# Moving operand splits, a butterfly step and gate copies between engines, and re-ordering the Fourier and gate stages of a hybrid GLA + Fourier encoder layer

## The chip, the cores and the metric

The kernel runs on one core of a Trainium2 chip. The metric is the device time of one execution in microseconds, the median of several. Five engines work side by side, each through its own instruction queue in order: PE (TensorE, matrix products), DVE (VectorE), ACT (ScalarE), POOL (GpSimd) and SP (SyncE, which here only starts DMAs).

## The reference, cut to what matters

```
proj = x @ w_in                      # 2048 x 1024 by 1024 x 2592
q, k, v, gf, gb, z_gla, u, z_fnet = split(proj)
log_a(dir) = log_sigmoid(g(dir) @ w_up(dir) + b(dir)) / 16
o = GLA_chunked(q, k, v, log_a fwd) + flip(GLA_chunked(flipped, log_a bwd))   # 4 heads
y_gla = rmsnorm(o) * g * silu(z_gla)
uf = real(fft2(u over positions and 128 channels of each of 4 groups)) @ w_fnet[group]
y_fnet = uf * silu(z_fnet)
out = layernorm(2**0.25 * x + concat(y_gla, y_fnet) @ w_out)
```

All data are float32. To keep precision each operand of a large product is held as a high part `hi` (rounded to the matmul's format) and a low part `lo = x - hi`, and each product is three matmuls: hi*hi, hi*lo, lo*hi.

## The kernel before, in words

The positions are cut into 8 blocks of 256 (`BLK`), the model width into 8 pieces of 128. Four phases follow one another.

Phase 1 projects `z_gla`, `u` and `z_fnet` (the last two by Strassen-like products, `run` and `product`, in the order of `LAST` for the last quarter) and writes them to DRAM scratch (`u_d`, `zf_d`, `zg_d`).

Phase 2 runs two generators side by side. `qk_all` goes through the 8 blocks: `load_x` loads x in two halves and splits it (`split`, lines 56 and 59: `hi` on ACT, `lo` on the engine given, here GpSimd), and `qk_block` makes four pieces ("qk steps") of 24 matmuls each (line 87), 32 steps in all. `fnet_pe` does the Fourier part for 4 groups of channels: `fft(g)` loads a 16 x 128 tile from `u_d`, and does a 16-point butterfly in the free dimension, almost all of it on DVE (lines 456 to 510; the subtraction of line 457 on GpSimd), ending in four splits into `bhl`; `stage2` (line 563) multiplies by the twiddle-and-DFT table `et`, `mixdown` (lines 575 to 590) by the channel matrices, and `gate_f` (line 598, on GpSimd) multiplies by `zf` and stores to `mf_d`. The transform of group 0, three pieces of that of group 1 and the loading of the table `et` stand ahead of the loop; the loop then lets the Fourier generator begin after `WARM` = 6 qk steps, and advances it twice a step. From step 18 on `wvg_load` loads and splits the weights of v and of the gate into the space that the Fourier tiles leave (`wA`), one piece per step (`hi` on ACT, line 655, `lo` on GpSimd, line 656).

Phase 3 makes v, the decay gates and the chunked attention, block by block. `pw_part` and `pv_part` (line 94, 24 matmuls each) project one half block; `gate_evac` copies the low-rank gate columns out of PSUM (lines 700 to 702) into `rn`; `gates` transposes `rn` (line 725), multiplies by the up-projection (line 733), takes log-sigmoid (lines 735 to 739), scans (744, 746), subtracts the middle of the chunk (750), clips (751), keeps small columns in `cmid`, `cend`, `cst` (755 to 759) and takes two exponentials (761, 762). `scaled` (777) applies these to q and k. `gla_a` (785 to 794) makes scores and transposed keys, masks them on DVE (`at`, lines 791 and 792); `gla_b` (802 to 810) makes the state updates and the inner output. A block's `gla_a` and `gla_b` run in the next block's turn. `chain_f` does the state recurrence on GpSimd (984, 987).

Phase 4 normalises, gates, projects out (line 1008) and does the LayerNorm; the change doesn't touch it.

Instructions are written in program order and assigned to their engine by the code; a planner then fixes the order within each engine's queue ahead of the run, by a list schedule in which program order is the priority and an estimate of readiness decides. `issue_after(i)` pins instructions behind `i` in their queue. Tiles with one tag share `bufs` buffers, so a load waits until the last reader of the buffer's previous content is done: `xraw` has 2 buffers, `xhl` 4, `wraw` 4.

Of the kernel before, what the change touches and what calls it, by code (L numbers as in the profile page):

```python
# [31 lines left out]
MID = 63  # L32
WARM = 6
LIMIT = 28.0
NS = 6
PRE = 3
LAST = ((0, 1), (0, 2), (0, 6), (0, 5), (0, 3), (1, 1), (1, 6), (0, 7), (0, 4), (1, 7), (1, 4), (1, 5), (1, 3), (1, 2))
CAP = (LIMIT + 1.0) * TAU
# [6 lines left out]
class Kern:  # L45
# [37 lines left out]
    def proj_t(self, ps, xh, w, c0):  # L83
        for k in range(KB):
            x = xh[k // 4]
            for i, (s, m) in enumerate(((0, 0), (0, 1), (1, 0))):
                self.nc.tensor.matmul(ps, w[:, s, k, c0:c0 + P], x[:, m, k % 4, :],  # L87
                                      start=(k == 0 and i == 0), stop=(k == KB - 1 and i == 2))

# [49 lines left out]
    def phase1(self):  # L139
# [3 lines left out]
        with ExitStack() as ctx:  # L143
# [252 lines left out]
            for p in range(NP):  # L396
                for _ in nxt:
                    pass
                nxt = x_prep(p + 1, xs[p + 1]) if p + 1 < NP else iter(())
                seq = both(p, (1, 2) + ORDER)  # L400
                if p == NP - 1:
                    seq = [(u, c, p) for u, c in LAST]
                for n, (u, c, _) in enumerate(seq):
                    run(u, c, p, xs[p])
                    if len(seq) - n in (9, 5, 3, 1):
                        next(nxt, None)
                    if p == NP - 1 and (u, c) == (0, 5):
                        self.wqk = self.load_w("wC", a["w_qk"], KB, 512)
                if p == 1:
                    self.consts()  # L410

    def consts(self):
# [20 lines left out]
    def phase2(self):  # L433
        nc, a = self.nc, self.a
        with ExitStack() as ctx:
# [10 lines left out]
            fw = self.wpool.tile([P, 56, P], F32, name="fw", tag="wA")  # L446

            def fft(g, out):
                V = nc.vector
                u = fw[:, 16 * (g % 2):16 * (g % 2) + 16]  # L450
                n = 4 if g == 0 else NCH
                for b in range(0, NCH, n):
                    nc.sync.dma_start(out=u[:, b:b + n], in_=self.u_d[:, b:b + n, g * P:(g + 1) * P])
                eo = fw[:, 32:48]
                tm = fw[:, 48:56]
                V.tensor_tensor(out=eo[:, 0:8], in0=u[:, 0:8], in1=u[:, 8:16], op=ALU.add)
                nc.gpsimd.tensor_tensor(out=eo[:, 8:16], in0=u[:, 0:8], in1=u[:, 8:16], op=ALU.subtract)
                yield
# [63 lines left out]

            bt0 = []
            for _ in fft(0, bt0):
                pass
            nb1 = []
            nf1 = fft(1, nb1)
            for _ in range(PRE):
                next(nf1)
            et = self.wpool.tile([P, 2, 9, 384], F32R, name="et", tag="wB")  # L530
            for k in range(9):
                raw = self.xpool.tile([P, 384], F32, name="eraw", tag="wraw", bufs=4)
                nc.sync.dma_start(out=raw, in_=a["etab"][:, k])
                self.split(et[:, 0, k], et[:, 1, k], raw)

            def qk_block(b, xh):
                for c0, d in ((256, self.kr_d[b]), (0, self.qr_d[b])):
                    ps = self.mm([P, 2, BLK])
                    for i in range(2):
                        self.proj_t(ps[:, i], xh, self.wqk, c0 + i * P)  # L540
                        if i == 0:
# [51 lines left out]
            def gate_f(g, yf):  # L593
                for b in range(NBLK):
                    zf = fp.tile([P, BLK], F32, name="zfl", tag="zfl", bufs=3)
                    nc.sync.dma_start(out=zf, in_=self.zf_d[b][:, g, :])
                    yb = yf[:, b * BLK:(b + 1) * BLK]
                    nc.gpsimd.tensor_tensor(out=yb, in0=yb, in1=zf, op=ALU.mult)
                    if b % 2:
# [3 lines left out]
            def fnet_pe():  # L603
                bt = bt0
                for _ in range(WARM):
                    yield
                pend = None
                for g in range(4):
# [4 lines left out]
                    for ks in ((1, 2), (3, 4), (5, 6), (7,), (0, 8)):  # L613
                        yhl = stage2(g, bt, ks)
                        next(nf, None)
# [14 lines left out]
            def qk_all():  # L630
                xn = self.load_x(0, nc.gpsimd)
                for b in range(NBLK):
                    xh = xn
                    if b + 1 < NBLK:
                        xn = self.load_x(b + 1, nc.gpsimd)
                    yield from qk_block(b, xh)

            ga, gb = qk_all(), fnet_pe()
            def wvg_load():
                w = self.wvg = self.wpool.tile([P, 2, KB, 544], F32R, name="wA_w", tag="wA")  # L640
                raws = []
                for k in range(KB + 4):
# [29 lines left out]
    def phase3(self):  # L672
# [16 lines left out]
        with ExitStack() as ctx:  # L689
# [28 lines left out]

            def gates(b, blk):
                rn = blk["rn"]  # L720
                tp = self.pg([P, 2, P])
                R = gp.tile([98, BLK], F32R, name="R", tag="R", bufs=1)
# [3 lines left out]
                nc.scalar.copy(out=R[0:96], in_=tp[0:96].rearrange("p t j -> p (t j)"))  # L726
                g = gp.tile([P, 4, BLK], F32, name="g", tag="g", bufs=2)
                zs = []
                for i in range(2):
# [24 lines left out]
                cs_ = slice(2 * b, 2 * b + 2)  # L754
                V.tensor_copy(out=cmid[:, cs_], in_=cv[:, :, :, MID])  # L755
                V.tensor_copy(out=cend[0:64, cs_], in_=gv[0:64, :, :, P - 1])
                V.tensor_copy(out=cend[64:128, cs_], in_=gv[64:128, :, :, 0])
                V.tensor_copy(out=cst[0:64, cs_], in_=gv[0:64, :, :, 0])
                V.tensor_copy(out=cst[64:128, cs_], in_=gv[64:128, :, :, P - 1])
                eq = c  # L760
# [62 lines left out]

            prev, xn = None, self.load_x(0, nc.gpsimd)
            for b in range(NBLK):
# [3 lines left out]
                pw_part(xh, 1, blk)  # L829
                gates(b, blk)  # L830
                qk_load(b, blk)
                if b + 1 < NBLK:
                    xn = self.load_x(b + 1, nc.gpsimd)
                if b < 2:
                    pv_part(xh, 0, blk)
                if b == 0:
                    pv_part(xh, 1, blk)
                if prev:
                    gla_a(b - 1, 0, prev)
                    if b > 1:  # L840
                        pv_part(xh, 0, blk)
                    gla_b(b - 1, 0, prev)
                scaled(blk)
# [324 lines left out]
```

## Time and profile before

| | |
|---|---|
| median of 3 runs | 863.68 us (863.08 to 865.26) |
| the profiled execution | 860.85 us, span of its instructions 859.1 us |
| PE busy | 788.5 us, 92% |
| DVE busy | 561.5 us, 65% |
| ACT busy | 381.7 us, 44% |
| POOL busy | 309.1 us, 36% |

Busy time is the time in which an engine executes; PE is counted busy at either level of its clock, which the profile gives as a granted share of full speed (1.00 is 2.4 GHz, 0.50 is 1.2 GHz, a value between is a mix in time). Times in the rows are microseconds from the span's start, mean durations are nanoseconds. "idle before <- X" names what ended an engine's idle time.

### The profile page before, as it was taken

To read this page: it belongs to the slowest core of one execution; us is meant where nothing else is said; L and a number is where in the kernel's file an instruction comes from. 1 tells how busy PE (TensorE), PEld (TensorE's weight loads), DVE (VectorE), ACT (ScalarE), POOL (GpSimd) and SP (SyncE) were. 2 spreads that over 40 slices of the span, in tenths; PEclk is the share of its full clock that TensorE was granted. 3 is DMA by queue.
4 is the path that set the end of the run, shared out by engine and by line. 5 is a ranking of instruction groups with operands and counts; after the bars stand their busy time and mean duration, and the time that the engine had idled before them with its cause. 6 is when DMAs were issued, how large, how long until landed. Compare 5 with 4: busy or idle time off the path is not lost. (4 is left out here: it accounts for less than half of the span.)

```text
span 859.1 us, 14088 instructions
## 1 busy us (share of the span) xinstructions
PE 788.5 (92%) x5542; PEld 737.1 (86%) x5542; DVE 561.5 (65%) x782; ACT 381.7 (44%) x668; POOL 309.1 (36%) x193
## 2 busy tenths in 40 slices
PE   7999999999999779799967979888988999999995
PEld 7999999999998769799966879887966788888885
DVE  5772377555458997642046788887796877677764
ACT  5864452332134234344244546545665444433441
POOL 0000003111123646357642464354344554455421
PEclk9999999999999789999978999898989999999998
DMA  8864345141338635366842543343448434554232
GB/s 246 276 221 129 110 151 175 64 143 62 118 123 257 203 126 169 121 192 198 235 148 74 147 130 114 91 141 117 123 133 284 167 134 150 186 196 147 89 109 78
DMA packets 75233, 130.51 MB, mean 152 GB/s; under 512 B 7219, under 2 KB 46643, under 8 KB 75158
## 3 DMA queue, kind: packets, MB, share of 16 engines
q1 hardware_dynamic: 72854, 125.34, 46.0%
q10 hardware_dynamic: 2304, 4.20, 1.4%
q8 instruction: 45, 0.74, 0.4%
q14 instruction: 30, 0.25, 0.1%
HBM read 92.81 MB, written 36.70 MB: 151 GB/s over the span
## 5 line engine op out<-in xcount | busy, mean ns | idle before, releaser
L94 PE MATMUL mm<-wA_w,xhl 128*128 128x272 f32 x768 | 111.6, 306 | 1.2 <-POOL xhl L59 1.2
L59 POOL TENSOR_TENSOR xhl<-xraw,xhl 128x1024 fp32r<-128x1024 f32 x32 | 83.9, 2626 | 73.1 <-ACT xhl L56 53.5
L94 PEld LDWEIGHTS mm<-wA_w,xhl 128*128 128x128 f32 x768 | 107.1, 205 | 1.7 <-POOL xhl L59 1.4
L87 PE MATMUL mm<-xhl,wC_w 128*128 128x256 f32 x768 | 101.5, 292 | 6.1 <-POOL xhl L59 6.1
L87 PEld LDWEIGHTS mm<-xhl,wC_w 128*128 128x128 f32 x768 | 98.7, 201 | 7.2 <-POOL xhl L59 6.6
L1008 PE MATMUL mm<-wB_w,mix 128*128 128x512 f32 (+1 forms) x396 | 94.6, 388 | 3.6 <-ACT mix L56 2.4
L1008 PE MATMUL mm<-wA_w,mix 128*128 128x512 f32 (+1 forms) x396 | 94.4, 391 | 2.1 <-ACT wA_w L56 2.1
L1008 PEld LDWEIGHTS mm<-wB_w,mix 128*128 128x128 f32 x396 | 73.1, 190 | 19.9 <-ACT mix L56 3.0
L984 POOL TENSOR_TENSOR S<-S 64x512 f32<-64x512 f32 x30 | 50.0, 1668 | 100.6 <-ACT S L804 94.8
L1008 PEld LDWEIGHTS mm<-wA_w,mix 128*128 128x128 f32 x396 | 72.3, 190 | 15.9 <-ACT wA_w L56 2.3
L87 PE MATMUL mm<-xhl,wA_w 128*128 128x256 f32 x672 | 81.3, 283 | 0.5 <-ACT zs L235 0.5
L87 PEld LDWEIGHTS mm<-xhl,wA_w 128*128 128x128 f32 x672 | 80.8, 192 | 1.1 <-ACT zs L235 0.7
L382 POOL TENSOR_TENSOR t<-t,t 128x512 f32<-128x512 f32 x7 | 11.0, 1576 | 191.8 <-ACT t L381 191.8
L56 ACT CAST xhl<-xraw 128x1024 fp32r<-128x1024 f32 (+1 forms) x54 | 51.4, 951 | 50.0 <-DMA xraw<-in_xt_dram 34.1
L1096 POOL TENSOR_TENSOR r<-r,lnb 128x1024 f32<-128x1024 f32 x15 | 35.8, 2387 | 78.2 <-issue 51.2
L59 DVE TENSOR_TENSOR x<-xraw,x 128x1024 fp32r<-128x1024 f32 x28 | 37.5, 1349 | 29.6 <-ACT x L56 29.6
L56 ACT CAST x<-xraw 128x1024 fp32r<-128x1024 f32 x28 | 29.0, 1047 | 44.2 <-PE mm L320 37.5
L320 PE MATMUL mm<-wC_s,x 128*128 128x256 f32 x384 | 48.2, 283 | 0.0
L320 PEld LDWEIGHTS mm<-wC_s,x 128*128 128x128 f32 x384 | 47.0, 192 | 0.0
L987 POOL TENSOR_TENSOR S<-S,alpha 64x512 f32<-64x512 f32 x30 | 44.5, 1483 | 2.3
L59 DVE TENSOR_TENSOR xhl<-xraw,xhl 128x1024 fp32r<-128x1024 f32 (+1 forms) x22 | 20.4, 932 | 28.6 <-ACT xhl L56 28.6
L320 PE MATMUL mm<-x,wB_s 128*128 128x256 f32 x288 | 36.5, 283 | 0.0
(183 smaller groups left out, 1520.5 us busy)
## 6 DMA issues: line engine op xcount, KB each, us to landing
xraw<-in_xt_dram SPq DMA_DIRECT2D x62, 512.0 KB, 4.6
xr<-in_x_dram SPq DMA_DIRECT2D x16, 512.0 KB, 3.7
out_dram<-r SPq DMA_DIRECT2D x15, 512.0 KB, 2.8
zg_d<-zs SPq DMA_DIRECT2D x32, 128.0 KB, 3.6
u_d<-t SPq DMA_DIRECT2D x16, 256.0 KB, 2.7
zf_d<-t SPq DMA_DIRECT2D x16, 256.0 KB, 2.1
zfl<-zf_d SPq DMA_DIRECT2D x32, 128.0 KB, 3.1
mf_d<-yf SPq DMA_DIRECT2D x16, 256.0 KB, 2.8
```

Source lines behind the costliest of these rows:

```text
L56: nc.scalar.copy(out=hi, in_=src)
L59: (lo_eng or nc.vector).tensor_tensor(out=lo, in0=src, in1=f32(hi), op=ALU.subtract)
L87: self.nc.tensor.matmul(ps, w[:, s, k, c0:c0 + P], x[:, m, k % 4, :], start=(k == 0 and i == 0), stop=(k == KB - 1 and i == 2))
L94: self.nc.tensor.matmul(ps, x[:, s, k % 4, t * P:(t + 1) * P], w[:, m, k, c0:c0 + cols], start=(k == 0 and i == 0), stop=(k == KB - 1 and ...
L320: nc.tensor.matmul(ps[:, i], s_[s][:, k, i * P:(i + 1) * P], m_[m][:, k], start=(k == 0 and j == 0), stop=(k == 3 and j == 2))
L382: G.tensor_tensor(out=T(3), in0=T(2), in1=T(0), op=ADD)
L984: E.tensor_tensor(out=S[ds, dst], in0=S[ds, dst], in1=S[ds, src], op=ALU.add)
L987: E.tensor_tensor(out=d3, in0=d3, in1=al, op=ALU.mult)
L1008: nc.tensor.matmul(y, c["mix"][:, s, eb], w[:, v, eb % 4, lo:lo + m], start=(eb == 4 and i == 0), stop=(eb == 3 and i == 2))
L1096: nc.gpsimd.tensor_tensor(out=r, in0=r, in1=lnb, op=ALU.add)
```

## The change

Five things change. (1) The `lo` halves of the splits of x in phases 2 and 3, the `lo` halves of the v and gate weights, the butterfly's subtraction and the gating of the last Fourier group go from GpSimd to VectorE. (2) Seven small copies per block of phase 3 go from VectorE to ScalarE. (3) The first transform and the loading of `et` are no longer ahead of the loop of phase 2: a generator `prelude` does them in pieces, two per step, beside `WARM` = 11 qk steps; their loads (`fft_load(0)`, `load_x(0)`) are issued in the last products of phase 1, two of which change places. (4) `stage2`'s matmuls are pinned behind the latest qk step's; the weights are loaded from step 24 on, two pieces a step, and the Fourier generator advances three times a step from step 27. (5) In phase 3 the transposes of `rn` become `gate_t`, and for blocks 2 to 7 the order is pw, pw, gla_a, gate_t, gla_b, gates, pv instead of pw, pw, transposes and gates, gla_a, pv, gla_b.

```diff
-WARM = 6
+WARM = 11
-PRE = 3
-LAST = (..., (1, 6), (0, 7), (0, 4), (1, 7), (1, 4), (1, 5), (1, 3), (1, 2))
+LAST = (..., (1, 6), (0, 7), (1, 7), (0, 4), (1, 4), (1, 5), (1, 3), (1, 2))
...
+                    if p == NP - 1 and (u, c) == (1, 4):
+                        self.fw = self.wpool.tile([P, 56, P], F32, name="fw", tag="wA")
+                        self.fft_load(0)
+                    if p == NP - 1 and (u, c) == (1, 3):
+                        self.x0 = self.load_x(0)
...
+    def fft_load(self, g):
+        u = self.fw[:, 16 * (g % 2):16 * (g % 2) + 16]
+        n = 4 if g == 0 else NCH
+        for b in range(0, NCH, n):
+            self.nc.sync.dma_start(out=u[:, b:b + n], in_=self.u_d[:, b:b + n, g * P:(g + 1) * P])
...
-                nc.gpsimd.tensor_tensor(out=eo[:, 8:16], in0=u[:, 0:8], in1=u[:, 8:16], op=ALU.subtract)
+                V.tensor_tensor(out=eo[:, 8:16], in0=u[:, 0:8], in1=u[:, 8:16], op=ALU.subtract)
...
-            for _ in fft(0, bt0):
-                pass
-            for _ in range(PRE):
-                next(nf1)
-            for k in range(9):
-                raw = self.xpool.tile([P, 384], F32, name="eraw", tag="wraw", bufs=4)
-                nc.sync.dma_start(out=raw, in_=a["etab"][:, k])
-                self.split(et[:, 0, k], et[:, 1, k], raw)
+            def et_load(ks):
+                for k in ks:
+                    raw = self.xpool.tile([P, 384], F32, name="eraw", tag="wraw", bufs=4)
+                    nc.sync.dma_start(out=raw, in_=a["etab"][:, k])
+                    self.split(et[:, 0, k], et[:, 1, k], raw)
+                    yield
+            def prelude():
+                yield from fft(0, bt0)
+                yield from et_load((1, 2, 3, 4, 5))
+                yield next(nf1)
+                yield from et_load((6, 7, 0, 8))
+                yield next(nf1)
+                yield next(nf1)
...
-                    nc.gpsimd.tensor_tensor(out=yb, in0=yb, in1=zf, op=ALU.mult)
+                    (nc.gpsimd if g < 3 else nc.vector).tensor_tensor(out=yb, in0=yb, in1=zf, op=ALU.mult)
...
+                pre = prelude()
                 for _ in range(WARM):
+                    next(pre, 0)
+                    next(pre, 0)
                     yield
+                for _ in pre:
+                    pass
...
-                        yhl = stage2(g, bt, ks)
+                        with self.tc.issue_after(self.qk_mm.ins):
+                            yhl = stage2(g, bt, ks)
...
-                xn = self.load_x(0, nc.gpsimd)
+                xn = self.x0
...
-                        xn = self.load_x(b + 1, nc.gpsimd)
+                        xn = self.load_x(b + 1)
...
-                        nc.gpsimd.tensor_tensor(out=lo, in0=raw, in1=f32(hi), op=ALU.subtract)
+                        nc.vector.tensor_tensor(out=lo, in0=raw, in1=f32(hi), op=ALU.subtract)
...
-                if step >= 18:
+                if step >= 24:
+                    next(gw, 0)
                     next(gw, 0)
...
-                for _ in range(2 if step > WARM else 1):
+                for _ in range(1 if step <= WARM else 2 if step < 27 else 3):
...
-                V.tensor_copy(out=rn[:, t, 64:96], in_=rn[:, t, 0:32])
+                nc.scalar.copy(out=rn[:, t, 64:96].bitcast(F32R), in_=sl)
...
-                V.tensor_copy(out=cmid[:, cs_], in_=cv[:, :, :, MID])
+                nc.scalar.copy(out=cmid[:, cs_], in_=cv[:, :, :, MID])
...
-            prev, xn = None, self.load_x(0, nc.gpsimd)
+            prev, xn = None, self.load_x(0)
...
-                gates(b, blk)
                 qk_load(b, blk)
                 if b + 1 < NBLK:
-                    xn = self.load_x(b + 1, nc.gpsimd)
-                if b < 2:
+                    xn = self.load_x(b + 1)
+                if b > 1:
+                    gla_a(b - 1, 0, prev)
+                    gate_t(blk)
+                    gla_b(b - 1, 0, prev)
+                    gates(b, blk)
                     pv_part(xh, 0, blk)
-                if b == 0:
-                    pv_part(xh, 1, blk)
-                if prev:
-                    gla_a(b - 1, 0, prev)
-                    if b > 1:
-                        pv_part(xh, 0, blk)
-                    gla_b(b - 1, 0, prev)
+                else:
+                    pv_part(xh, 0, blk)
+                    gate_t(blk)
+                    if b == 0:
+                        pv_part(xh, 1, blk)
+                    else:
+                        gla_a(b - 1, 0, prev)
+                        gla_b(b - 1, 0, prev)
+                    gates(b, blk)
                 scaled(blk)
```

(The copies to `cend` and `cst`, four a block, change engine like that to `cmid`. `gate_t` holds the transposes and the copy of `R` that stood at the head of `gates`.)

## Rows read from the trace of the kernel before

**Rows 1.** The page's first part: busy us, share of the span, instructions.

```profile
PE 788.5 (92%) x5542; PEld 737.1 (86%) x5542; DVE 561.5 (65%) x782; ACT 381.7 (44%) x668; POOL 309.1 (36%) x193
```

**Rows 2.** Busy time by stage: PE, PEld, DVE, ACT, POOL, then PEclk, DMA share, GB/s.

```profile
264.60:350.00 85.40, 68.71 (x499) 66.10 (x498) 79.67 (x156) 30.39 (x52) 45.03 (x21) 0.89 0.57 181
264.60:421.50 156.90, 140.15 (x1086) 137.40 (x1085) 103.50 (x204) 61.44 (x107) 86.70 (x58) 0.93 0.59 181
421.50:438.25 16.75, 7.55 (x52) 6.39 (x50) 1.27 (x6) 3.94 (x8) 12.51 (x14) 0.87 0.78 234
438.25:489.60 51.35, 44.32 (x288) 41.22 (x288) 36.66 (x44) 23.54 (x45) 18.24 (x8) 0.84 0.35 110
489.60:514.90 25.30, 20.93 (x176) 19.67 (x175) 21.28 (x24) 14.22 (x27) 13.08 (x6) 1.00 0.40 117
489.60:615.80 126.20, 113.26 (x871) 106.42 (x870) 103.57 (x122) 70.27 (x135) 57.54 (x28) 0.92 0.41 121
615.80:637.00 21.20, 16.99 (x135) 15.39 (x134) 19.05 (x25) 14.09 (x26) 7.31 (x4) 0.88 0.16 47
```

**Rows 3.** Timeline of PE in phase 2: start, us, line, count, idle before.

```profile
281.82 2.93 PE L87 MATMUL mm<-xhl,wC_w 128*128 128x256 f32 x12 [3.48 <-POOL xhl L59]
...
308.39 1.44 PE L583 MATMUL pg<-yhl,wcs 128*128 128x256 f32 x5 [3.51 <-DVE yhl L59]
...
407.12 14.56 PE L87 MATMUL mm<-xhl,wC_w 128*128 128x256 f32 x120
```

**Rows 4.** Groups by line and form, 264.6 to 421.5: busy us, mean ns, idle.

```profile
L59 DVE TENSOR_TENSOR bhl<-fw,bhl 128x512 fp32r<-128x512 f32 x16 | 23.6, 1491 | 0.8 <-ACT bhl L56 0.7
L465 DVE SCALAR_TENSOR_TENSOR fw<-fw 128x128 f32<-128x128 f32 x80 | 18.4, 299 | 0.0
L468 DVE TENSOR_TENSOR fw<-fw 128x512 f32<-128x512 f32 x8 | 10.7, 1362 | 0.0
L59 DVE TENSOR_TENSOR yhl<-pa,yhl 128x512 fp32r<-128x512 f32 x16 | 11.0, 686 | 12.3 <-ACT yhl L56 12.2
L59 POOL TENSOR_TENSOR xhl<-xraw,xhl 128x1024 fp32r<-128x1024 f32 x16 | 42.2, 2644 | 40.6 <-ACT xhl L56 31.8 <-DMA zfl<-zf_d 8.8
L457 POOL TENSOR_TENSOR fw<-fw 128x1024 f32<-128x1024 f32 x4 | 13.5, 3367 | 8.5 <-DMA wraw<-in_w_vg_dram 7.8 <-DMA fw<-u_d 0.6
```

**Rows 5.** SP's waits, 264 to 421: us in total, times, longest.

```profile
SPq L77 <- POOL xhl L59: 41.1, 12, 8.4
```

**Rows 6.** Timeline of DVE: an undisturbed split, and four beside GpSimd's.

```profile
198.30 1.22 DVE L59 TENSOR_TENSOR x<-xraw,x 128x1024 fp32r<-128x1024 f32 x1
279.89 10.73 DVE L59 TENSOR_TENSOR bhl<-fw,bhl 128x512 fp32r<-128x512 f32 x4 [0.33 <-ACT bhl L56]
```

**Rows 7.** ScalarE at the start of phase 3.

```profile
428.54 1.05 ACT L56 CAST xhl<-xraw 128x1024 fp32r<-128x1024 f32 x1 [11.47 <-DMA xraw<-in_xt_dram]
```

**Rows 8.** The chain of waits through one block of phase 3.

```profile
514.95 0.45 PE mm L733 x2
...
526.28 0.93 DVE cmid L755
...
530.31 6.02 PE mm L94 x48
...
536.57 2.67 DVE rn L701
...
540.83 0.51 PE mm L733
```

**Rows 9.** Groups by line and form, 489.6 to 615.8 (five blocks).

```profile
L701 DVE COPY rn<-rn 128x32 f32<-128x32 f32 x10 | 14.8, 1479 | 6.2 <-ACT rn L700 6.2
L777 DVE TENSOR_TENSOR kx<-kx,g 128x1024 f32<-128x1024 f32 x5 | 14.1, 2820 | 0.5
L702 DVE TENSOR_TENSOR rn<-mm,rn 128x32 fp32r<-128x32 f32 x10 | 1.8, 178 | 0.0
L700 ACT CAST rn<-mm 128x32 fp32r<-128x32 f32 x10 | 1.8, 180 | 1.2 <-PE mm L94 1.0
```

**Rows 10.** Timeline of GpSimd beside the small copy of one block.

```profile
536.87 2.33 POOL L59 TENSOR_TENSOR xhl<-xraw,xhl 128x1024 fp32r<-128x1024 f32 x1
```

More of the change, by code (lines that the diff above doesn't have):

```diff
@@ L32 @@
 MID = 63
-WARM = 6
+WARM = 11
 LIMIT = 28.0
 NS = 6
-PRE = 3
-LAST = ((0, 1), (0, 2), (0, 6), (0, 5), (0, 3), (1, 1), (1, 6), (0, 7), (0, 4), (1, 7), (1, 4), (1, 5), (1, 3), (1, 2))
+LAST = ((0, 1), (0, 2), (0, 6), (0, 5), (0, 3), (1, 1), (1, 6), (0, 7), (1, 7), (0, 4), (1, 4), (1, 5), (1, 3), (1, 2))
 CAP = (LIMIT + 1.0) * TAU
@@ L86, in proj_t @@
             for i, (s, m) in enumerate(((0, 0), (0, 1), (1, 0))):
-                self.nc.tensor.matmul(ps, w[:, s, k, c0:c0 + P], x[:, m, k % 4, :],
-                                      start=(k == 0 and i == 0), stop=(k == KB - 1 and i == 2))
+                mm = self.nc.tensor.matmul(ps, w[:, s, k, c0:c0 + P], x[:, m, k % 4, :],
+                                           start=(k == 0 and i == 0), stop=(k == KB - 1 and i == 2))
+        return mm
     def proj_n(self, ps, xh, w, t, c0, cols, ks=range(KB)):
@@ L445, in phase2 @@
                 self.split(wcs[i][0], wcs[i][1], ps)
-            fw = self.wpool.tile([P, 56, P], F32, name="fw", tag="wA")
+            fw = self.fw
             def fft(g, out):
@@ L450, in fft @@
                 u = fw[:, 16 * (g % 2):16 * (g % 2) + 16]
-                n = 4 if g == 0 else NCH
-                for b in range(0, NCH, n):
-                    nc.sync.dma_start(out=u[:, b:b + n], in_=self.u_d[:, b:b + n, g * P:(g + 1) * P])
+                if g:
+                    self.fft_load(g)
                 eo = fw[:, 32:48]
@@ L521, in fft @@
                     yield
-            bt0 = []
-            for _ in fft(0, bt0):
-                pass
-            nb1 = []
+            bt0, nb1 = [], []
             nf1 = fft(1, nb1)
-            for _ in range(PRE):
-                next(nf1)
             et = self.wpool.tile([P, 2, 9, 384], F32R, name="et", tag="wB")
-            for k in range(9):
-                raw = self.xpool.tile([P, 384], F32, name="eraw", tag="wraw", bufs=4)
-                nc.sync.dma_start(out=raw, in_=a["etab"][:, k])
-                self.split(et[:, 0, k], et[:, 1, k], raw)
+            def et_load(ks):
[11 more added lines that the diff above has]
+                yield next(nf1)
             def qk_block(b, xh):
@@ L539, in qk_block @@
                     for i in range(2):
-                        self.proj_t(ps[:, i], xh, self.wqk, c0 + i * P)
+                        self.qk_mm = self.proj_t(ps[:, i], xh, self.wqk, c0 + i * P)
                         if i == 0:
@@ L717, in pv_part, with gate_t @@
                 nc.scalar.copy(out=blk["v"][t][:, 0:272], in_=pv)
-            def gates(b, blk):
+            def gate_t(blk):
                 rn = blk["rn"]
                 tp = self.pg([P, 2, P])
-                R = gp.tile([98, BLK], F32R, name="R", tag="R", bufs=1)
+                R = blk["R"] = gp.tile([98, BLK], F32R, name="R", tag="R", bufs=1)
                 nc.vector.memset(f32(R[96:98]), 1.0)
@@ L726, in gates @@
                 nc.scalar.copy(out=R[0:96], in_=tp[0:96].rearrange("p t j -> p (t j)"))
+            def gates(b, blk):
+                R = blk["R"]
                 g = gp.tile([P, 4, BLK], F32, name="g", tag="g", bufs=2)
-                zs = []
                 for i in range(2):
@@ L754, in gates @@
                 cs_ = slice(2 * b, 2 * b + 2)
-                V.tensor_copy(out=cmid[:, cs_], in_=cv[:, :, :, MID])
[L756 to L759, printed above, removed]
+                nc.scalar.copy(out=cmid[:, cs_], in_=cv[:, :, :, MID])
+                nc.scalar.copy(out=cend[0:64, cs_], in_=gv[0:64, :, :, P - 1])
+                nc.scalar.copy(out=cend[64:128, cs_], in_=gv[64:128, :, :, 0])
+                nc.scalar.copy(out=cst[0:64, cs_], in_=gv[0:64, :, :, 0])
+                nc.scalar.copy(out=cst[64:128, cs_], in_=gv[64:128, :, :, P - 1])
                 eq = c
```

## The prediction

> **What bounds the kernel now.** I read the page's totals first, then the busy time by stage, then the timelines and the chain inside the stages that are not full. By the totals PE works 92% of the span and nothing else passes 65% [rows 1], so what can be won is PE's idle time and the time in which it runs at half clock. The stages say where that is [rows 2]. Before 264.6 the first phase keeps PE busy, and behind 637 the last phase runs on code that isn't touched. Two stretches lose time: phase 2 (264.6 to 421.5) and phase 3 (421.5 to 637).
>
> Phase 2: at full clock a matmul of 256 columns takes 0.12 us, from 120 of them between 407.12 and 421.52 [rows 3]. The 1086 matmuls of the stretch are then 130.3 us of work, and it takes 156.9 [rows 2], so 26.6 us are lost. The timeline shows the losses in gaps of 3.5 us: first PE waits for a GpSimd half of x, later for VectorE's Fourier splits, and each gap has a stretch at lower clock behind it (12 matmuls of 0.12 take 2.93) [rows 3]. VectorE is the reason on paper: 79.7 of the 85.4 us to 350 it is busy [rows 2]. But much of that isn't work. A 128x512 operation with one input in PSUM takes 0.686 us on it, the splits into bhl, of the same size but with both inputs in SBUF, take 1.491 on average [rows 4], and four that fall beside GpSimd's splits take 10.73 together [rows 6].
>
> Phase 3: in the block from 489.6 to 514.9 the clock is 1.00 all through and PE is busy 20.93 us of 25.3. I take 20.93 as a block's work. Five blocks take 126.2 [rows 2] where that is 104.7: 21.5 us lost. The chain shows how a block's turn closes: gate product at 514.95, VectorE's scans, the subtraction, the copy cmid (0.93), masks, 6.02 us of projection, then a copy of 128x32 that takes 2.67 us, and only then the next gate product at 540.83 [rows 8]. That copy is 0.18 us of work, if the neighbouring operation of the same form is a measure; the mean over ten is 1.479 [rows 9]. It starts at 536.57, and GpSimd's split runs from 536.87 to 539.20 [rows 10]; the copy ends with it.
>
> The Trainium skill states the reason for such pairs ("SBUF — State Buffer", section "SBUF: two separate sides"): GpSimd and VectorE share a port pair as an exclusive lock, taken by a VectorE operation in a two-port mode or with two SBUF inputs, and the loser waits for the whole instruction. By that rule the trace agrees: 2.67 against 0.18, and 10.73 for four. By it the excess in bhl comes back with GpSimd's splits gone and the forecast's sum holds; without it none comes back, and the sum is that of rival 4.
>
> **The change part by part.** All sums stand on the profiled execution: span 859.1, time 860.85; the median of the runs shown, 863.68, is 2.8 us above that, and I carry the difference over.
>
> (a) Splits off GpSimd in phase 2. Sixteen splits of x (42.2 us) and four subtractions (13.5) leave GpSimd [rows 4]. On VectorE each is one 128x1024 operation; undisturbed it takes 1.22 us [rows 6], so it gains 20 x 1.22 = 24.4 us. What it gets back: 16 x (1.491 - 0.686) = 12.9 from bhl and 8 x (1.362 - 0.686) = 5.4 from the first butterflies [rows 4], 18.3 in these two rows alone, in so far as gate_f, which stays on GpSimd for three groups, doesn't take it again. Weight splits (8 or 9 of 0.69 each by the same size) and the last gating (eight operations of half that size) fall behind 350, where VectorE has 103.5 - 79.7 = 23.8 us of work in 71.5 [rows 2]: hidden there. All in all VectorE has some 103.5 + 24.4 + 9 - 18.3 = 119 us of work in phase 2 against PE's 130.3. It fits, closely.
>
> (b) SP's queue. SP waited 41.1 us in 12 waits for GpSimd to free an xraw buffer [rows 5], and loads, stores and table pieces behind that wait stood too. A split of 1.22 behind ScalarE's half frees it sooner. The moved issues (four loads of u, two of x, in phase 1's tail) stand ahead of the last stores of zf, which nobody reads before the first gate_f; the swap in LAST makes the last u product one place later, 24 x 0.12 = 2.9 us, while the loads of u wait for it. I cost this at nothing; its cover is the x block already split when phase 2 begins, and without it the first step stands for one gap of 3.5 [rows 3].
>
> (c) The transform beside eleven steps. Twelve steps of 24 matmuls keep PE for 34.6 us. VectorE must in that time do the first transform (2 operations of 1.22 [rows 6], 20 of 0.30, six of 0.69 [rows 4] and eight smaller ones of at most that: 13 to 18), three blocks of x (6 x 1.22 = 7.3), the table (9 pieces of at most 0.69: 6) and the first pieces of the second transform (4 to 6): 30 to 37. So the two sides are level. The new wait is the pin: stage2 stands in PE's queue behind a qk step, and everything on PE stands behind stage2. If bhl is late the price is one gap of 3.5 and its half clock each time.
>
> Of the 26.6 lost in phase 2 I take back 21: the gaps for GpSimd's halves go entirely, those for Fourier splits mostly; one or two gaps stay, since VectorE is near full. Ends: 26.6 if all goes, 10 if the Fourier gaps stay.
>
> (d) The start of phase 3, to the third gate product at 489.6. From 421.5 it takes 16.75 + 51.35 = 68.1 us for 52 + 288 matmuls [rows 2]; at the 20.93 / 176 of the full-clock block that is 40.4, so 27.7 are lost. ScalarE's queue shows one reason: an x split stands 11.47 us for its DMA [rows 7] with a copy of qk results and the gate columns behind it. The buffer comes free earlier with VectorE's splits, and the products of v fill the wait for the transposes. On the other side the weights now begin six steps later, and the end of the Fourier part comes closer to the end of phase 2, so its stores can hold phase 3's memory. I take 13, about half; ends 3 (the contention alone) and 24.
>
> (e) Blocks 2 to 7. Off the chain go the copy of 2.67 (a ScalarE copy of about 0.18 takes its place [rows 9]), and cmid, 0.93 [rows 8]: 2.49 + 0.93 = 3.4. The second copy of the pair, also slow on average, was beside PE's work. On the chain come up to four ScalarE copies ahead of the exponentials, 4 x 0.18 = 0.7, though VectorE's copies stood in the same place ahead of `scaled`; kx's product drops from 2.82 to 1.22 [rows 9, 6], and two splits of 1.22 come onto VectorE. With gla_a ahead of the transposes PE has work while the gate columns are copied. I take 3 us a block, 15 for five; ends: the whole 21.5, and a loss of 6 if both new splits and the copies fall in the chain: 5 x (2 x 1.22 + 0.7 + 1.5 - 3.4) = 6, where 1.5 is half of kx's surplus, kept because the state chain stays on GpSimd. Queue cover: ScalarE has 70.27 us of work in 126.2 [rows 2], seven more copies a block are 6.3 in all.
>
> (f) The last block, 615.8 to 637: the cmid copy, about 1 us. From 637 to the end nothing.
>
> Sum: 21 + 13 + 15 + 1 = 50. Span 809, profiled time 811, median 863.7 - 50 = 814.
>
> **The rivals.**
> 1. *The gate chain goes on pacing phase 3.* z, scans, exponentials and `scaled` are untouched and the new order puts a product that needs `scaled` ahead of the transposes. For it: the scans and products stand in the chain of every block [rows 8]. Against: half of what the chain waits for is GpSimd [rows 10]. Then (d) gives 3 and (e) 5: 863.7 - 21 - 3 - 5 - 1 = 834; with fewer gaps filled in phase 2, up to 848.
> 2. *PE becomes full.* All losses go: 26.6 + 24 + 21.5 + 1 = 73: 791. For it: one block already runs at clock 1.00 [rows 2]. Against: the chain, and VectorE level with PE in (c).
> 3. *The plan doesn't come out.* Weights late, or the pinned stage2 finding its splits late again and again; the gaps return and the time is 848 to 866. By the gaps of [rows 3], eight of them with half clock behind eat the 40.
> 4. *Slower: VectorE becomes the bound.* Its place is the first 85 us of phase 2, where it is busy 93% [rows 2], and the price is what it is given and doesn't get back. If the long bhl durations are its own and not GpSimd's, 24.4 us come on top, less the 5.7 it has free: +18.7; the pin passes each delay to PE. In phase 3 two splits a block, 2.44, less the copies it loses, 7 x 0.18 = 1.3, come to +1.2 a block in a chain that then keeps its 2.67: +8 in seven. 863.7 + 27 = 890. It decides where bhl's splits stay near 1.49 with GpSimd's splits gone, that is where nothing of the 24.4 comes back. Against it: the same operation takes 1.22 where GpSimd is still and the excess falls exactly beside it [rows 6, 10].
>
> **How the numbers follow.** Chances: forecast 0.55 (own range 800 to 829), rival 1 0.18, rival 2 0.14, rival 3 0.07, rival 4 0.06. A measurement of this kernel tells a change from none at about 0.3%, 2.6 us, so "same" is 861.1 to 866.3; of rival 3 some 0.03 falls there. Faster 0.91, same 0.03, slower 0.06. The range 792 to 848 holds the forecast, rival 1 and about half of rival 2; the chances outside come to some 0.2.
>
> **What would show it.** (a) right: bhl near 0.7 us each and no PE gap that ends on GpSimd's x; wrong: bhl still above 1.2. (c): PE in one piece from 266 to 300. Phase 2 to end near 400; (d) the third gate product near 455; (e) gate products 22 us apart and the gate copies at 0.18 on ScalarE; phase 3 to end near 587. The prediction is wrong if the first weights product waits for its weights, if PE still stands for masks or gate columns for over 2 us a block, or if the clock between 490 and 616 stays near 0.92.

## The result and the profile after

The kernel after takes 835.66 us (median of 4, 834.93 to 842.69), the one before beside it 864.47: ratio 0.967 [0.961, 0.974]. The forecast of 814 was 22 us low. Of the 50 us of the sum 29 came, and the 834 of rival 1 is nearest; whether its mechanism was the right one is what the experiments are about. The profiled execution is the slowest of the four (842.69, clock 0.969; the other three 834.9 to 836.1 at 0.976 to 0.979), so its span of 840.9 stands 18.2 below that of before, where the medians stand 29 apart. The stages below are those of the two profiled executions; the other 11 us of the gain lie in executions of which there is no trace.

The totals of the page, which answer to [rows 1]:

```profile
PE 778.9 (93%) x5542; PEld 729.8 (87%) x5542; DVE 551.7 (66%) x779; ACT 388.9 (46%) x724; POOL 189.8 (23%) x140
```

GpSimd lost 119 us of work, and VectorE, which took most of it over, is 10 us less busy than before. The stages, to set against [rows 2] (phase 1, phase 2, from its end to the third gate product, from there to the eighth gate product; columns as there):

```profile
0.00:267.58 267.58, 259.70 (x2112) 258.77 (x2113) 145.08 (x166) 118.12 (x190) 21.96 (x19) 0.99 0.49 155
267.58:404.97 137.39, 132.20 (x1086) 130.48 (x1085) 112.08 (x238) 61.88 (x107) 21.06 (x24) 1.00 0.64 202
404.97:467.57 62.60, 51.63 (x369) 48.59 (x367) 37.75 (x47) 29.44 (x71) 10.13 (x10) 0.86 0.55 160
467.57:600.00 132.43, 115.36 (x873) 108.83 (x872) 86.28 (x95) 75.08 (x171) 30.67 (x20) 0.91 0.42 116
```

Phase 1 ends 3.0 us later, phase 2 is 19.5 us shorter at clock 1.00, the start of phase 3 5.5 shorter (62.6 for 68.1), and the five blocks are 6.2 us *longer* (132.4 for 126.2); what follows the eighth gate product gives 2.4. That is the 18.2. The gate products don't mark quite the same place in both orders: 369 matmuls stand ahead of the third from the start of phase 3 where it was 340, and some 30 fewer behind the eighth. By the 20.93 us for 176 matmuls of a full-clock block these are about 3.4 us (an estimate), so for equal work the start of phase 3 gained nearer 9 us than 5.5, and the end lost about 1 instead of gaining 2.4.

In phase 2 the picture is the one forecast. The timeline of PE, and the group of the bhl splits (for [rows 3, 4]):

```profile
268.90 35.12 PE L86 MATMUL mm<-xhl,wC_w 128*128 128x256 f32 x288
...
346.38 0.62 PE L599 MATMUL pg<-yhl,wcs 128*128 128x256 f32 x3 [2.75 <-DVE yf L606]
```

```profile
L58 DVE TENSOR_TENSOR bhl<-fw,bhl 128x512 fp32r<-128x512 f32 x16 | 11.1, 707 | 0.2
```

PE runs through the twelve steps in one piece, its longest later gap in the phase is 2.75 us, and a bhl split takes 0.707 us where it took 1.491.

In the blocks the copies are as short as forecast, and still the block is longer. One block, from the gate product at 493.76 to the next at 520.96, by the timelines of ScalarE, VectorE, GpSimd and PE (for [rows 8 to 10]):

```profile
504.03 0.20 ACT L780 COPY cmid<-c 128x8 f32<-128x8 f32 x1 [2.25 <-DVE c L771]
504.14 0.38 ACT L740 COPY v<-mm 128x272 f32<-128x272 f32 x1
504.42 1.05 ACT L55 CAST xhl<-xraw 128x1024 fp32r<-128x1024 f32 x1
505.36 0.58 ACT L829 COPY S<-pg 64x512 f32<-64x512 f32 x1
...
508.72 0.20 ACT L781 COPY cend<-g 64x8 f32<-64x8 f32 x1 [1.56 <-DVE g L776]
...
509.39 0.20 ACT L784 COPY cst<-g 64x8 f32<-64x8 f32 x1
509.62 1.06 ACT L786 ACTIVATE c<-g 128x1024 f32<-128x1024 f32 x1
```

```profile
501.71 2.29 DVE L771 TENSOR_TENSOR_SCAN c<-rst,g 64x1024 f32<-64x1024 bf16 x1
504.03 0.73 DVE L817 COPY_PREDICATED at<-mb,pa 128x512 f32<-128x512 uint8 x1
504.65 1.21 DVE L775 TENSOR_TENSOR g<-c 128x1024 f32<-128x1024 f32 x1
...
506.91 1.78 DVE L776 TENSOR_SCALAR g<-g 128x1024 f32<-128x1024 f32 x1
512.13 1.79 DVE L802 TENSOR_TENSOR kx<-kx,g 128x1024 f32<-128x1024 f32 x1 [0.19 <-ACT g L787]
```

```profile
506.08 2.05 POOL L1014 TENSOR_TENSOR S<-S 64x512 f32<-64x512 f32 x1 [9.81 <-ACT S L829]
510.92 1.92 POOL L1017 TENSOR_TENSOR S<-S,alpha 64x512 f32<-64x512 f32 x1 [2.78 <-ACT alpha L846]
```

```profile
493.76 0.72 PE L758 MATMUL mm<-R,wg 98*128 98x256 f32 x4
504.90 1.13 PE L834 MATMUL pg<-at,v 128*128 128x128 f32 x8 [1.82 <-DVE at L817]
505.79 6.25 PE L94 MATMUL mm<-wA_w,xhl 128*128 128x272 f32 x48
513.97 0.37 PE L810 MATMUL pa<-qp,kx 64*128 64x128 f32 x1 [1.93 <-DVE kx L802]
520.96 1.20 PE L758 MATMUL mm<-R,wg 98*128 98x256 f32 x4
```

```profile
512.04:513.97 1.93, 0.00 (x1) 0.00 (x0) 1.84 (x2) 0.21 (x3) 0.80 (x1) 1.00 0.63 240
513.97:520.96 6.99, 6.99 (x42) 6.28 (x43) 1.66 (x4) 2.91 (x8) 0.60 (x1) 0.60 0.31 86
```

Read it from cmid. The copy lasts 0.20 us, but it waits for the second scan (L771) at the head of ScalarE's queue, and the copies of the state update into S (L829) stand behind it. So GpSimd's state step (L1014) begins at 506.08, in the middle of the gate chain, and the clip beside it (L776) takes 1.78 us; its second half falls beside the keys' product, 1.79. Between the clip and the exponential (L786) stand four copies, 0.9 us together. PE waits twice for VectorE, 1.82 us for a mask and 1.93 for the scaled keys, and behind the second wait its granted clock is 0.60: the scores, transposes and updates from there to the next gate product take 6.99 us.

### The profile page after: what moved, and what is told of

Same layout as the page of the kernel before. It is cut to its first block, busy times and chain, and to the rows that moved or that the text cites. A ratio compares the mean times of both kernels' runs of the same rounds, so it can differ in the third digit from the quotient of the medians.

```text
span 840.9 us, 14089 instructions
## 1 busy us (share of the span) xinstructions
PE 778.9 (93%) x5542; PEld 729.8 (87%) x5542; DVE 551.7 (66%) x779; ACT 388.9 (46%) x724; POOL 189.8 (23%) x140
## 4 chain that ended last, share of the span: by engine, by line
PE 59%; DVE 16%; DMA 10%; ACT 8%; issue 6%; POOL 1%; SPq 1%; ACTq 0%; DVEq 0%; POOLq 0%
PE mm L1038 18%; PE mm L320 15%; PE mm L86 12%; DMA xraw<-in_xt_dram 2%; DVE c L771 2%; PE mm L94 2%; PE pa L1078 2%; PE pa L810 2%; PE pa L579 2%; DVE fw L478 2%; DMA fw<-u_d 2%; DVE fw L475 1%; PE pg L827 1%; DVE g L776 1%; DMA zfl<-zf_d 1%
## 5 line engine op out<-in xcount | busy, mean ns | idle before, releaser
L94 PE MATMUL mm<-wA_w,xhl 128*128 128x272 f32 x768 | 105.7, 297 | 0.0
L94 PEld LDWEIGHTS mm<-wA_w,xhl 128*128 128x128 f32 x768 | 102.2, 196 | 0.0
L86 PE MATMUL mm<-xhl,wC_w 128*128 128x256 f32 x768 | 96.0, 284 | 0.0
L86 PEld LDWEIGHTS mm<-xhl,wC_w 128*128 128x128 f32 x768 | 93.7, 192 | 0.5 <-issue 0.5
L58 DVE TENSOR_TENSOR xhl<-xraw,xhl 128x1024 fp32r<-128x1024 f32 (+1 forms) x54 | 61.0, 1132 | 31.9 <-ACT xhl L55 31.6
L1014 POOL TENSOR_TENSOR S<-S 64x512 f32<-64x512 f32 x30 | 43.3, 1445 | 144.8 <-ACT S L829 138.7
L55 ACT CAST xhl<-xraw 128x1024 fp32r<-128x1024 f32 (+1 forms) x54 | 51.4, 953 | 35.9 <-DMA xraw<-in_xt_dram 18.2
L614 POOL TENSOR_TENSOR yf<-yf,zfl 128x256 f32<-128x256 f32 x24 | 21.1, 896 | 126.2 <-ACT yf L593 113.4
```

What stands on the lines that cost most here:

```text
L55: nc.scalar.copy(out=hi, in_=src)
L58: (lo_eng or nc.vector).tensor_tensor(out=lo, in0=src, in1=f32(hi), op=ALU.subtract)
L86: mm = self.nc.tensor.matmul(ps, w[:, s, k, c0:c0 + P], x[:, m, k % 4, :], start=(k == 0 and i == 0), stop=(k == KB - 1 and i == 2))
L94: self.nc.tensor.matmul(ps, x[:, s, k % 4, t * P:(t + 1) * P], w[:, m, k, c0:c0 + cols], start=(k == 0 and i == 0), stop=(k == KB - 1 and ...
L614: (nc.gpsimd if g < 3 else nc.vector).tensor_tensor(out=yb, in0=yb, in1=zf, op=ALU.mult)
L1014: E.tensor_tensor(out=S[ds, dst], in0=S[ds, dst], in1=S[ds, src], op=ALU.add)
```

## The experiments

Ratios are against the kernel before, timed beside it on the same chip. "Period" is the mean distance of the third to the eighth gate product in the profiled execution (25.2 before, 26.5 after).

**The kernel after once more.** 

> The changed kernel once more, nothing edited, as the control of this group and for a second profile (the profiled execution of the first was 842.7 us, the timed ones about 835). Both theories: 835 us. Theory A (the new order closes a loop: the next block's gate product stands on TensorE behind the state products, which need this block's scaled keys): gate products 26 to 27 us apart again, 25.2 before. Rival B (the work moved onto VectorE and ScalarE, two splits and five copies a block, lengthens the gate chain): the same distance.

 Measured: 840.0 us (833.8 to 841.9), 0.969 [0.963, 0.974]; period 26.5.

**Old order in phase 3.**
```diff
+                gate_t(blk)
+                gates(b, blk)
                 qk_load(b, blk)
...
                     gla_a(b - 1, 0, prev)
-                    gate_t(blk)
+                    if b > 1:
+                        pv_part(xh, 0, blk)
                     gla_b(b - 1, 0, prev)
-                    gates(b, blk)
-                    pv_part(xh, 0, blk)
```


> The changed kernel with only the order of phase 3 put back (pw, pw, transposes and gates, pv, gla_a, gla_b); copies stay on ScalarE, splits on VectorE. Theory A: the loop through the scaled keys opens, the gate products come about 22.7 us apart (25.9 of the old chain less 2.5 for the gate copy and 0.9 for cmid), some 3.7 us less for six blocks: 813 to 820 us. Rival B: the added VectorE and ScalarE work is still in the chain, distance 25 to 27 us, 830 to 840 us.

 Measured: 831.8, 0.962 [0.957, 0.966]; period 24.1. The direction is theory A's, the size is not: the new order costs some 2.4 us a block *in this kernel*, but without it the block is still above the 22.7 that theory A named, and the time lies in rival B's range. Nor is the 2.4 a price of the order alone, since the clock differs too; the last experiment has blocks of the new order at clock 1.00, and they take 24.6.

**Phase 3 as before, phases 1 and 2 as after.** 

> The changed phases 1 and 2 with phase 3 wholly as before: order, copies on VectorE, splits on GpSimd. It prices phase 3's part. Phase 2 ends some 19 us earlier than before. Theory A and B alike, if phase 3's net gain is as small as the first trace makes it look (about 5 us): 840 to 847 us. If phase 3's edits were worth the 29 us forecast in parts (d) to (f): 865.

 Measured: 847.3, 0.980 [0.975, 0.985]; period 25.2. So the first two phases are worth 18.5 us, and all of phase 3's part some 7 to 12 (against 840.0 and 835.7); both theories had said 840 to 847.

**Splits of x in phase 3 on GpSimd.**
```diff
-                    xn = self.load_x(b + 1)
+                    xn = self.load_x(b + 1, nc.gpsimd)
```


> The changed kernel with only the splits of x in phase 3 put back on GpSimd. Theory A: the loop stays, two splits of 1.2 us leave VectorE's chain but GpSimd's of 2.4 us block it instead; gate products 26 to 28 us apart, 833 to 845 us. Rival B: without the two splits in VectorE's queue the distance falls by up to 2.4 us, 821 to 830 us.

 Measured: 849.7, 0.981 [0.976, 0.986]; period 27.6. Rival B is refuted for the splits: back on GpSimd they cost 10 us against 840.0, a little more than theory A's range.

**The seven copies back on VectorE.**
```diff
-                nc.scalar.copy(out=rn[:, t, 64:96].bitcast(F32R), in_=sl)
+                V.tensor_copy(out=rn[:, t, 64:96], in_=rn[:, t, 0:32])
-                nc.scalar.copy(out=cmid[:, cs_], in_=cv[:, :, :, MID])
+                V.tensor_copy(out=cmid[:, cs_], in_=cv[:, :, :, MID])
...
```
The four lines of cend and cst change alike. 

> The kernel after, with the seven small gate copies of a block (two roundings of the gate products, cmid, cend, cst) made on VectorE as before; order, splits and phases 1 and 2 stay. Theory C, the copies had been long only because they stood beside GpSimd's splits: with the splits off GpSimd they should take under 0.3 us each on VectorE, some 1.5 us a block, and they leave a ScalarE that took 4 in a row at 0.2 us; 838 to 846 us, block loop at 26 to 27.5 us a block. Rival D, the copies on ScalarE are what brought the gain of the block loop: 2.5 us a block and more come back, 852 us or more.

 Measured: 827.4 (825.9 to 828.6), 0.955 [0.953, 0.958]; period 24.0. Both C and D fail: the copies are indeed short on VectorE (0.16 us for cmid), but ScalarE had not *brought* a gain, it had cost 10 to 11 us by the ratios. No outcome that I had written down was on that side.

**zf loaded ahead.** The last Fourier group's zf rows go into a free buffer of the tag yf instead of three small ones. 

> The kernel after, with the rows zf of the last Fourier group loaded into a buffer that stands free then instead of three small buffers of blocks, so that the transform's products of that group do not wait for them. Theory E, the 13.9 us for which the first rounding of phase 3 waits on a transfer of the Fourier results (yf to mf_d) end early because these loads stand behind the stores on SP's queue: the first gate product comes at 412 to 417 us instead of 422, and 832 to 836 us in all against 840. Rival F, other memory of phase 2 ends as late, or the block loop takes the gain up: first product later than 419 us, and a time within 0.3% of the kernel after.

 Measured: 839.8, 0.969 [0.967, 0.972]: rival F. The first rounding's wait for the stores of yf fell from 13.9 to 9.4 us and the second gate product came 3.3 us earlier, but the first stayed at 422.0 (24 products of v now stood ahead of it) and the third at 467.2.

**Both masks ahead of the scans.**
```diff
+                gate_t(blk)
...
                     gla_a(b - 1, 0, prev)
...
+                    gla_a(b - 1, 1, prev)
+                gates(b, blk)
+                pv_part(xh, 0, blk)
...
                     gla_b(b - 1, 0, prev)
...
+                pv_part(xh, 1, blk)
                 scaled(blk)
```
(The lines that these replace are left out.) 

> The kernel after with another order in phase 3's blocks: both products of masked scores of the block before come ahead of this block's gate scans, so that VectorE masks them before it starts the scans, and no product of TensorE that needs these masks stands behind the scans. Theory A: the loop over scaled keys, transposes and the next gate product opens; a block takes 21 to 23.5 us instead of 26.5, and the time comes to 812 to 825 us. Rival G, VectorE has no slack left: the masks that now stand ahead of the scans delay the gates by their 3.3 us a block, the loop stays above 25 us a block, and the time is 835 us or more.

 Measured: 858.3, 0.992 [0.989, 0.995]; period 28.6. Theory A's forecast for it was wrong by 33 us, and both numbers are rival G's. Its mechanism, masks that delay the gates by 3.3 us, is not what the trace shows: from a gate product (472.07) to the end of the keys' product it is 20.6 us for 20.2 in the kernel after. My edit put a second product that needs scaled keys ahead of the gate product, and from the keys' product's end (492.67) to the gate product (500.94) it is 8.3 us instead of 7.0, at a clock of 0.53. The loop that theory A names is there, and this edit lengthened it; the clock over the five blocks is 0.80, where it was 0.91, and how much of the 2.1 us a block is the clock's was not separated. **With zf ahead as well:** 

> The two edits before this one together: the zf rows loaded ahead, and both masks ahead of the scans. If theories A and E both hold, their gains add, as one acts before the third gate product and the other behind it: the time is that of the masks-first kernel less 4 to 8 us. If E's gain is taken up by the block loop, it is within 2 us of the masks-first kernel alone.

 Measured: 855.0, 0.987 [0.985, 0.990], 3.3 us below: between the two outcomes written down.

**Old order and VectorE copies.** The edits of the second and the fifth experiment together. 

> The kernel after with phase 3's old order of the products and with the seven small gate copies on VectorE: the fourth cell of order and copies (new order and ScalarE copies 840, old order and ScalarE copies 832, new order and VectorE copies 827). Theory H, order and copies meet in one wait, the one for the scaled keys, and each alone takes it away: no further gain, 824 to 832 us, 23.5 to 24.3 us a block. Rival J, they are two costs that add: 8 us and 12 us less than the kernel after, 816 to 821 us, under 23 us a block.

 Measured: 829.2, 0.960 [0.956, 0.964]; period 23.7. Theory H: the two costs don't add. With the copies on VectorE the new order is 2 to 4 us better than the old by medians and ratios, with overlapping intervals.

**cmid alone on VectorE** (one line of the diff above). 

> The kernel after with one of the seven copies, cmid, on VectorE; the six others stay on ScalarE. Theory K, cmid is what costs: on ScalarE it stands behind the second scan and holds the copies into S behind it, so that GpSimd's state step falls beside the clip of the gates (1.78 us instead of 0.68) and the next beside the keys' product (1.79 instead of 1.22). With it on VectorE the copies into S come ahead of the scans' end, clip is near 0.7, and the time is 828 to 833 us. Rival L, the four copies cend and cst, 0.9 us ahead of the exponentials, are the price: no more than 3 us are won, 836 to 841 us.

 Measured: 830.4 (826.2 to 832.0), 0.961 [0.958, 0.964]; period 24.1. **cend and cst alone on VectorE** (four lines). 

> The kernel after with the four copies cend and cst of a block on VectorE; cmid and the gate columns' copies stay on ScalarE. Theory K: the S copies still stand behind cmid, clip stays near 1.8 us, and 0.9 us a block at most is won: 834 to 840 us. Rival L: the first exponential starts as soon as clip ends, the wait for the keys' product goes, and the time is 826 to 832 us.

 Measured: 825.3 (824.5 to 825.7), 0.955 [0.951, 0.958]; period 24.2. K and L are each right on its own kernel and wrong on the other: either edit takes the extra time away. For the first of the two, its timelines of VectorE, GpSimd and PE, and two stretches by engine:

```profile
498.02 1.87 DVE L775 TENSOR_TENSOR g<-c 128x1024 f32<-128x1024 f32 x1
...
501.02 0.68 DVE L776 TENSOR_SCALAR g<-g 128x1024 f32<-128x1024 f32 x1
505.13 1.79 DVE L802 TENSOR_TENSOR kx<-kx,g 128x1024 f32<-128x1024 f32 x1 [0.19 <-ACT g L787]
```

```profile
497.54 1.26 POOL L1014 TENSOR_TENSOR S<-S 64x512 f32<-64x512 f32 x1 [7.91 <-ACT S L829]
```

```profile
498.27 1.13 PE L834 MATMUL pg<-at,v 128*128 128x128 f32 x8 [1.82 <-DVE at L817]
```

```profile
505.30:506.90 1.60, 0.10 (x1) 0.00 (x0) 1.60 (x2) 0.00 (x0) 0.53 (x1) 1.00 0.75 284
506.90:511.38 4.48, 4.41 (x42) 3.98 (x43) 1.73 (x5) 2.33 (x8) 0.00 (x0) 1.00 0.44 136
```

The state step is over before the clip, and the clip takes 0.68 instead of 1.78. But the step now falls beside the subtraction ahead of it, which takes 1.87 instead of 1.21, so 0.4 us of the 1.1 is left. The wait for the keys is still there, 1.60 us for 1.93, the mask's wait is the same 1.82; the clock holds at 1.00, and the stretch that took 6.99 us takes 4.48. In the other kernel the clip stays at 1.77 and the exponential starts right behind it:

```profile
498.12 1.77 DVE L776 TENSOR_SCALAR g<-g 128x1024 f32<-128x1024 f32 x1
```

```profile
499.99 1.06 ACT L786 ACTIVATE c<-g 128x1024 f32<-128x1024 f32 x1 [1.62 <-DVE g L776]
```

The wait for the keys goes, but for two of 2.0 us in sum where the kernel after has five of 9.2 (PE's waits from 465 to 600, after and then this one):

```profile
PE pa L810 <- DVE kx L802: 9.2, 5, 1.9
```

```profile
PE pa L810 <- DVE kx L802: 2.0, 2, 1.1
```

**Phase 2's splits back on GpSimd**, its new schedule kept (`nc.gpsimd` in `load_x`, the butterfly's subtraction and the weights' `lo`; the two splits of the first block of x, which phase 1 loads, stay on VectorE, so 14 of 16 go back). 

> The kernel after with the splits of phase 2 (16 of x, the weights' eight) and the four Fourier subtractions back on GpSimd; the new schedule of phase 2 and all of phase 3 stay. Step (a) of the prediction: bhl goes back to 1.3 to 1.5 us each, PE waits for GpSimd's halves again, phase 2 takes 148 us or more against 137, and the time is 8 to 18 us above the kernel after. Rival M, the schedule alone (the transform in pieces beside eleven steps) is what shortened phase 2: under 142 us, and a time within 4 us of the kernel after.

 Measured: 851.9, 0.985 [0.982, 0.988]. Phase 2 takes 152.4 us, 15 more than after, and the splits are long again:

```profile
L58 POOL TENSOR_TENSOR xhl<-xraw,xhl 128x1024 fp32r<-128x1024 f32 x14 | 42.7, 3058 | 21.9 <-ACT xhl L55 21.9
L58 DVE TENSOR_TENSOR bhl<-fw,bhl 128x512 fp32r<-128x512 f32 x16 | 18.3, 1155 | 0.5 <-ACT bhl L55 0.2
```

So of the 19.5 us of phase 2, 15 hang on the engine of the splits and 4.5 are what the new schedule gives without them; rival M is refuted. A bhl split at 1.155 is a little under the 1.3 expected.

Phase 3 is not edited in this kernel, and its blocks show whether the longer wait for the keys is what lowers the clock. Two of its blocks in a row, by PE's waits for VectorE (one mask and one keys' product each), as whole blocks, and by the stretch behind the keys' wait:

```profile
520.05 1.13 PE L834 MATMUL pg<-at,v 128*128 128x128 f32 x8 [1.82 <-DVE at L817]
529.13 0.37 PE L810 MATMUL pa<-qp,kx 64*128 64x128 f32 x1 [1.94 <-DVE kx L802]
544.69 1.13 PE L834 MATMUL pg<-at,v 128*128 128x128 f32 x8 [1.82 <-DVE at L817]
553.76 0.37 PE L810 MATMUL pa<-qp,kx 64*128 64x128 f32 x1 [1.94 <-DVE kx L802]
```

```profile
508.91:533.54 24.63, 20.86 (x177) 19.79 (x176) 17.41 (x19) 15.13 (x35) 6.29 (x4) 1.00 0.44 129
533.54:560.73 27.19, 23.42 (x177) 22.06 (x176) 17.40 (x19) 15.71 (x35) 6.89 (x5) 0.90 0.41 117
529.13:533.54 4.41, 4.41 (x42) 3.99 (x43) 1.65 (x4) 2.34 (x8) 0.00 (x0) 1.00 0.42 137
553.76:560.73 6.97, 6.97 (x42) 6.26 (x43) 1.65 (x4) 2.91 (x8) 0.60 (x1) 0.61 0.26 83
```

The same block behind the same two waits takes 24.63 us at clock 1.00 and 27.19 where the clock falls to 0.61 behind the second. The block ahead of these two, from 484.28, also has waits of 1.81 and 1.94, takes 24.63 and stays at 1.00.

## Why the prediction was right or wrong

The time lies in the stated range, but not where the sum put it: the forecast's own range ended at 829, and the wide one holds the result because it holds rival 1. That the total comes within 2 us of rival 1's 834 is partly luck, since its terms for (d) and (e), gains of 3 and 5, were a gain of 5.5 and a loss of 6.2 in the profiled execution.

**(a) to (c), phase 2: right.** 19.5 us for the 21 of the sum, and for the reason given: bhl at 0.707, no PE gap that ends on GpSimd, the twelve steps in one piece, some gaps left (four, 5.2 us together, behind VectorE's yf). With GpSimd's splits gone bhl takes 0.707, and with them back 1.155. The Trainium skill's rule for the shared port pair ("SBUF — State Buffer", section "SBUF: two separate sides"), by which the one that comes second waits for the other's whole instruction, agrees with that in both directions. Against rival 4, VectorE did not become the bound: it is busy 112.1 us of the 137.4, where the forecast had 119. Phase 1, where (b) put its price at nothing, ends 3.0 us later. The moved loads and the swap in `LAST` can be only a small part of that: at 66 us, long before them, PE has done 439 matmuls for 459 before, which is 2.4 us at 0.12 each. The other kernels with this phase 1 end it between 265.5 and 269.1; how much of the 3.0 is no more than a difference between executions can't be told from one trace of before.

**(d), the start of phase 3: half.** 5.5 us of 13 in the profiled execution. The caveat in it, that the Fourier part's stores would hold phase 3's memory, came true: the first rounding on ScalarE waits 13.9 us for the stores of yf.

```profile
420.62 0.18 ACT L723 CAST rn<-mm 128x32 fp32r<-128x32 f32 x1 [13.92 <-DMA mf_d<-yf]
```

PE has products of v to do meanwhile and stands for 4.0 us of it, out of 11 in the stage; the rest of the loss is other waits and a clock of 0.86. Taking a third of the 13.9 away gained nothing by the median, so it was not the only holder. Part of the rest belongs to the copies of (e): from the first product of v to the third gate product it takes 62.6 us in the kernel after, 58.3 with cend and cst on VectorE, 60.6 with the old order.

**(e), the blocks: wrong, and in the profiled execution in sign.** The step says "On the chain come up to four ScalarE copies ahead of the exponentials, 4 x 0.18 = 0.7, though VectorE's copies stood in the same place", and puts "cmid, 0.93" off the chain. The durations were right (0.18 to 0.21 us each). What failed first is the price by duration. A copy moved to another engine brings its wait along: cmid waits for the scan at the head of ScalarE's in-order queue and delays what stands behind it, the copies into S, and through them GpSimd's step, which then meets the clip. The prediction's "Queue cover" counted ScalarE's sum of work (6.3 us more in 126) and not what is queued behind a waiting copy.

Rival 1 named what failed second: "the new order puts a product that needs `scaled` ahead of the transposes". So there is a loop, gate product to scaled keys (20.2 us after) and scaled keys to the next gate product (7.0), and its length is the block: 27.2. The sum took 3 us off the old chain as if no other closed the block. With cmid on VectorE the loop is 19.8 and 4.5. Of that difference 0.4 us is chain and 2.5 us is clock. At clock 1.00 the blocks say the same: 24.63 us with all copies on ScalarE (the two of the last experiment), 24.26 with cmid on VectorE, and 25.27 before the change (the one block there at 1.00). So moving the copies cost about 0.4 us a block directly, and where the clock holds the change as a whole wins 0.6 a block, for the 3 forecast.

The larger part of the loss is the clock, which stood at 0.91 over the five blocks; that it stays near 0.92 was one of the prediction's own signs of being wrong. What lowers it stays open. It is not alone the 0.33 us by which PE's waits are longer (3.75 in two for 3.42): behind the same waits it held twice and fell the third time. What the runs show is that in both profiles of the kernel after four of the five blocks ran at 0.87 to 0.93, while in the three kernels with copies back on VectorE no block was under 0.93 and the period is 24.0 to 24.2.

**The splits of phase 3** were worth their place: about 10 us, by the run that puts them back. With the copies on VectorE, splits and order give a period of 24.0, not 22: PE still waits for the second mask, behind the scans: 1.4 to 1.8 us a block in the kernel after, and 1.8 to 2.0 in most blocks of all five variants with a period near 24.

**(f)** 2.4 us came for the 1 forecast, but some 30 matmuls fewer lie in that stretch; for equal work it is a loss of about 1.

The best kernel of this study is the one after with cend and cst on VectorE: 825.3 us, 0.955 of before, 10 us or more under the change as it was made (835.7 and 840.0). That wait for the second mask and the start of phase 3 are where PE still stands; the one attempt at each (masks first, zf ahead) won nothing.

## What to carry to other kernels

Before moving a small operation to a less busy engine, find the event it waits for and list what stands behind it in that engine's queue; its own duration can be the smaller part of its price. When an order is changed, write down the loop that closes over one turn of it, engine by engine, and check that the moved product doesn't need the turn's last result. Where PE waits in short pieces, look at the granted clock behind each wait, block by block: here the same waits cost nothing more in one block and 2.6 us in the next.

## What the runs showed of the hardware

A VectorE operation with a single SBUF operand can be held by GpSimd as well: the clip of 128x1024 takes 0.68 us with GpSimd still and 1.78 beside a state step. One with two is held likewise: the scan of 64x1024 takes 2.29 and, beside GpSimd's steps in the two kernels with the old order and the splits on VectorE, 3.20 in most blocks. GpSimd pays too: its step of 64x512 takes 1.28 us with VectorE nearly still (493.87 in the kernel after) and 2.05 where it begins inside a split of VectorE's (506.08). Blocks of the same instructions behind the same waits ran at clock 1.00 and at 0.90, 24.6 and 27.2 us, in one execution. Two executions of one kernel differ by 8 us along with the clock: the kernel after took 834.9 at 0.977 and 842.7 at 0.969, while the version that hardly waits for its keys stayed within 1.2 us.
